# A hybrid decoder layer: projections that hand TensorE over at every second group of three matmuls

## The chip, the core and the metric

One core of a Trainium2 chip runs the whole layer as one program. The metric is the device time of one execution in microseconds (us), the median of several runs. The engines are named as the profile names them: PE is TensorE (PEld its weight loads), DVE VectorE, ACT ScalarE, POOL GpSimd, SP SyncE, whose queue issues most of the DMAs.

## What is computed

The input x is 512 tokens of 2048 numbers, all in float32. With the modulation left out, the layer is:

```
h = rmsnorm(x) * (1 + sc_m) + sh_m
proj = h @ w_in                      # 2048 x 8208
o_hg  = hgrn2_group(proj[:, :4096])  # 8 heads: q, f, i, g of 128 columns each
o_gdn = gdn_group(proj[:, 4096:])    # 8 heads: q, k, v, g of 128 columns each
y = concat(o_hg, o_gdn) @ w_out
x = x + gt_m * rmsnorm(y)
...                                  # then the MLP with w_ff1 and w_ff2
```

Each HGRN2 head is a gated linear recurrence over the tokens. Each Gated DeltaNet head needs a triangular solve for every chunk and then a recurrence from chunk to chunk:

```
v_new = u_c - w_c @ S
o = qd_c @ S + qk_c @ v_new
S = S * tail + kt_c^T @ v_new
```

## The kernel before, in words

Large products run as three matmuls for each pair of 128x128 weights and 128x512 activations: every float32 operand is split into a high part H and a low part L, and `mm3` issues H·H, H·L and L·H into one PSUM bank. A group of three matmuls below is one call of `mm3`. The weights come by DMA into `raw` tiles of 128x1024; ACT makes the high part (`wh`, L197) and DVE the low part (`wl`, L199), each split feeding eight groups.

The stage that the change touches is called the mixing here. It lasts from about 285 to 1095 us of the profiled execution. Its parts on TensorE are:

- Projections. For heads 2 to 7 there are eight columns per head, 48 in all, and `project` (L933) runs 16 groups for each into a bank `pj` (three banks). Then `out_mm` groups of the output projection follow (banks `pout`).
- The recurrences, in three threads, each a Python generator that yields the time that its next step should wait. `solve_thread` runs the triangular solve of one DeltaNet head: the matmuls `pk`, `pkk` and `pb`, and then 15 steps of substitution that are DVE work alone (L1032 and L1034, tiles `utmp` and `uc`). `gdn_thread` runs the rest of that head: `pqk`, two levels (`py`, `pz`), then four chunks with the matmuls `p1` (from the state S), `p2`, `p4` and `po`, and at the end four transposes `pog`. `hg_thread` runs an HGRN2 head: `pd`, seven levels `pa`, then chunks `hp` and `hpo`, and the transposes `poh`. The trace leaves numbers out, so `p1`, `p2` and `p4` are all `p` there and are told apart by what they read (S, R or U, vn).

Between two matmuls of one thread lies work on DVE, ACT and POOL. For one `p1` it is the update of S on DVE (L1146).

What sets the order: PE and SP are in program order (`manual_schedule`), and `run` writes that program. It keeps a clock of its own. It takes the first thread whose next step is due by that clock, and if none is due it takes one step of the filling work, `fill`, that is the projections and then the output projection. A step of a projection ends where the generator `project` yields, so a recurrence that falls due during a step waits until its end. DVE, ACT and POOL are ordered by the framework's scheduler, which follows the program, so their order moves with it.

At the end of the mixing `fill_thread` starts the output projection. Its last two pairs of heads need the transposes of DeltaNet head 7 (`pog7`, then L957 into `xo`, and the split of it into `oH` on ACT, L1418, and `oL` on DVE, L1419) and of HGRN2 head 7 (`poh7`, likewise).

Of the kernel before, what the change touches and what calls it, by code (L numbers as in the profile page):

```python
# [235 lines left out]
def hybrid_layer_kernel(  # L236
# [228 lines left out]
    def mm3(ps, aH, aL, bH, bL, start, stop):  # L465
        mm(ps, aH, bH, start, False)
        mm(ps, aH, bL, False, False)
        mm(ps, aL, bH, False, stop)
# [436 lines left out]
    def pj(name):  # L905
        return bank("pj", name)
# [26 lines left out]
    def project(col, out):  # L933
        ps = pj(f"pj{col}")
        for hf in range(2):
            wH, wL = ws.get(("in1", col, hf))
            for kk in range(8):
                kt = hf * 8 + kk
                mm3(ps, wH[:, kk, :], wL[:, kk, :], hH[:, kt, :], hL[:, kt, :], kt == 0, kt == KT - 1)
                yield 0  # L940
        out.append(ps)

    def finish_head(name, slot, osb, sso, nw, gate, rq=None):
# [415 lines left out]
    def fill_thread():  # L1359
# [29 lines left out]
        for h in range(2, NH):  # L1389
            todo = [(("grec", h - 2), gpre, C_GK, None), (("grec", h - 2), gpre, C_GQ, None),  # L1390
                    (("v", h - 1), gpre, C_GV, ("gpre", h)),
                    (("hrec", h - 1), hpre, C_HF, None), (("hrec", h - 1), hpre, C_HQ, None),
                    (("hv", h - 1), hpre, C_HI, ("hpre", h)),
                    (("gfin", h - 1), gpre, C_GG, ("gate_g", h)), (("hfin", h - 1), hpre, C_HG, ("gate_h", h))]
            for need, f, cc, tok in todo:
                yield from flush(PJ - 1)
                out = []
                yield from project(cc + h * P, out)
                pending.append((need, f, cc, h, out.pop(), tok, True))
# [404 lines left out]
```

## Time and profile before

| | |
|---|---|
| median of 3 runs | 2586.42 us (2584.91 to 2587.82) |
| the profiled execution's own time | 2583.66 us |
| its span in the profile | 2581.9 us |
| PE busy | 2469.1 us, 96% of the span, 12627 instructions |
| DVE busy | 1875.9 us, 73% |
| ACT, POOL busy | 1118.1 us (43%), 1032.4 us (40%) |
| DMA | 350.64 MB, 136 GB/s on the mean |

To read it: the page gives busy time per engine over the whole span, but the stages differ. In the MLP, from about 1262 to 2470 us, PE has no idle time at all; in the start and the mixing it has. So a share over the span says little about the mixing, and the rows further down are of that stretch. A matmul of 128x512 shows some 390 ns, but matmuls are pipelined and follow each other about every 227 ns. The idle time in brackets in a row of the timeline is the time in which the engine did nothing before that instruction, and behind the arrow stands what ended the wait.

### The profile page before, as it was taken

Reading aid. Unit: us, or ns where it says so; the run is one execution under the profiler, and the core shown is the slowest. Engines: PE = TensorE matmul, PEld = TensorE weight load, DVE = VectorE, ACT = ScalarE, POOL = GpSimd, SP = SyncE. Lnnn points to the kernel's source line nnn. Section 1 sums busy time; section 2 is a strip of 40 time slices with the busy share of each in tenths; the row PEclk is TensorE's granted clock in tenths of the full one; section 3 lists DMA queues with packets and bytes.
Section 4 is the critical chain, followed back from the end, with each engine's and each line's share of the span. In section 5 each row is a group of like instructions: output and inputs, shape, how many; then the busy total and the mean of one; then the engine's idle time right before and its main releaser. Section 6 shows DMA issues by size and latency. Waiting matters only on the chain.

```text
span 2581.9 us, 34110 instructions
## 1 busy us (share of the span) xinstructions
PE 2469.1 (96%) x12627; PEld 2007.2 (78%) x12627; DVE 1875.9 (73%) x2709; ACT 1118.1 (43%) x1765; POOL 1032.4 (40%) x646
## 2 busy tenths in 40 slices
PE   5889999998999899999999999999999999999998
PEld 3667777777777778788788888888888888888876
DVE  7997877768586765634668776777768777677787
ACT  5553544544444452423444444444434434443333
POOL 5561344445444440000244535445354444533333
PEclk9999999999999999999999999999999999999999
DMA  8762434444545432344423332433424333232334
GB/s 320 255 203 74 128 119 147 139 148 138 160 142 164 139 115 82 130 140 155 154 98 133 104 135 95 146 123 106 142 95 139 110 127 135 94 114 82 122 116 161
DMA packets 127300, 350.64 MB, mean 136 GB/s; under 512 B 14247, under 2 KB 18713, under 8 KB 125981
## 3 DMA queue, kind: packets, MB, share of 16 engines
q1 hardware_dynamic: 126938, 348.41, 40.0%
q8 instruction: 99, 1.62, 0.3%
q14 instruction: 67, 0.55, 0.1%
q10 hardware_dynamic: 196, 0.06, 0.0%
HBM read 340.01 MB, written 8.40 MB: 135 GB/s over the span
## 4 chain that ended last, share of the span: by engine, by line
PE 67%; DVE 6%; POOL 1%; ACT 1%; issue 1%; DMA 1%; DVEq 0%; ACTq 0%; POOLq 0%
PE pf L331 27%; PE pg L331 22%; PE pj L331 9%; PE pout L331 7%; DVE wl L199 1%; DVE uc L1034 1%; PE pa L331 1%; DVE utmp L1032 1%; POOL y L1728 0%; POOL aacc L451 0%; PE p L331 0%; DVE x2r L1746 0%; DMA ada<-in_w_ada_dram 0%; DVE zkT L493 0%; PE pz L331 0%
## 5 line engine op out<-in xcount | busy, mean ns | idle before, releaser
L199 DVE TENSOR_TENSOR wl<-raw,wh 128x1024 fp32r<-128x1024 f32 x506 | 720.1, 1424 | 427.8 <-ACT wh L197 422.6
L197 ACT CAST wh<-raw 128x1024 fp32r<-128x1024 f32 x512 | 538.0, 1052 | 943.4 <-PE pf L331 285.9
L165 POOL TENSOR_TENSOR raw<-raw,raw 128x1024 f32<-128x1024 f32 x150 | 438.9, 2941 | 392.7 <-DMA raw<-in_w_ff_dram 181.6
L331 PE MATMUL pf<-h2L,wh 128*128 128x512 f32 x1024 | 399.9, 391 | 0.0
L331 PE MATMUL pf<-h2H,wh 128*128 128x512 f32 x1024 | 399.7, 390 | 0.0
L331 PE MATMUL pf<-h2H,wl 128*128 128x512 f32 x1024 | 399.6, 390 | 0.0
L451 POOL TENSOR_TENSOR aacc<-ada,aacc 128x512 f32<-128x512 f32 x180 | 268.9, 1494 | 253.5 <-ACT ada L449 242.2
L331 PE MATMUL pg<-wl,cH 128*128 128x512 f32 x840 | 327.6, 390 | 1.1 <-DVE wl L199 1.1
L331 PE MATMUL pg<-wh,cL 128*128 128x512 f32 x840 | 327.3, 390 | 0.0
L331 PE MATMUL pg<-wh,cH 128*128 128x512 f32 x840 | 327.3, 390 | 0.0
L331 PE MATMUL pj<-hH,wh 128*128 128x512 f32 x768 | 325.2, 423 | 0.0
L331 PE MATMUL pj<-hH,wl 128*128 128x512 f32 x768 | 305.0, 397 | 4.4 <-DVE wl L199 4.4
L331 PE MATMUL pj<-hL,wh 128*128 128x512 f32 x768 | 304.0, 396 | 0.0
L331 PEld LDWEIGHTS pf<-h2H,wh 128*128 128x128 f32 x1024 | 192.7, 188 | 39.7
L331 PEld LDWEIGHTS pf<-h2L,wh 128*128 128x128 f32 x1024 | 192.7, 188 | 39.6
L331 PEld LDWEIGHTS pf<-h2H,wl 128*128 128x128 f32 x1024 | 192.7, 188 | 39.6
L451 POOL TENSOR_TENSOR gacc<-ada,gacc 128x512 f32<-128x512 f32 x64 | 108.4, 1694 | 278.9 <-ACT ada L449 278.9
L1627 DVE TENSOR_TENSOR y<-pg,y 128x512 f32<-128x512 f32 x344 | 219.0, 682 | 0.0
L331 PEld LDWEIGHTS pg<-wl,cH 128*128 128x128 f32 x840 | 157.8, 188 | 35.0 <-DVE wl L199 2.3
L331 PEld LDWEIGHTS pg<-wh,cH 128*128 128x128 f32 x840 | 157.8, 188 | 32.7
L331 PEld LDWEIGHTS pg<-wh,cL 128*128 128x128 f32 x840 | 157.8, 188 | 32.5
L331 PEld LDWEIGHTS pj<-hH,wl 128*128 128x128 f32 x768 | 146.4, 191 | 39.2 <-DVE wl L199 6.5
(434 smaller groups left out, 3770.3 us busy)
## 6 DMA issues: line engine op xcount, KB each, us to landing
raw<-in_w_ff_dram SPq DMA_DIRECT2D x256, 512.0 KB, 4.0
raw<-in_w_in_dram SPq DMA_DIRECT2D x128, 512.0 KB, 3.4
ada<-in_w_ada_dram SPq DMA_DIRECT2D x256, 256.0 KB, 3.4
adas<-in_w_ada_dram SPq DMA_DIRECT2D x128, 256.0 KB, 4.4
raw<-in_w_out_dram SPq DMA_DIRECT2D x40, 512.0 KB, 3.5
xo<-in_x_dram SPq DMA_DIRECT2D x8, 512.0 KB, 9.4
xr<-in_x_dram SPq DMA_DIRECT2D x8, 512.0 KB, 6.8
x2d<-z SPq DMA_DIRECT2D x4, 1024.0 KB, 5.7
```

The lines of the kernel that those rows point to most:

```text
L165: self.nc.gpsimd.tensor_tensor(out=out, in0=ra, in1=rb, op=op)
L197: self.cast = self.nc.scalar.copy(out=h, in_=raw).ins
L199: eng.tensor_tensor(out=lo, in0=raw, in1=h.bitcast(F32), op=ALU.subtract)
L331: nc.tensor.matmul(ps, lhsT=lhsT, rhs=rhs, start=start, stop=stop)
L451: nc.gpsimd.tensor_tensor(out=acc, in0=a, in1=acc, op=ALU.add)
L1032: nc.vector.tensor_tensor(out=tmp[:, :, :n], in0=xj, in1=uc[:, :, j : j + 1].broadcast_to([P, NCH, n]), op=ALU.mult)
L1034: nc.vector.tensor_tensor(out=uc[:, :, j + 1 :], in0=uc[:, :, j + 1 :], in1=tmp[:, :, :n], op=ALU.subtract)
L1627: nc.vector.tensor_tensor(out=dst, in0=ps, in1=dst, op=ALU.add)
```

## The change

`project` yields after every second group in place of every one, so `run` looks for a recurrence that is due half as often:

```
--- before.py
+++ after.py
@@ -937,7 +937,8 @@
             for kk in range(8):
                 kt = hf * 8 + kk
                 mm3(ps, wH[:, kk, :], wL[:, kk, :], hH[:, kt, :], hL[:, kt, :], kt == 0, kt == KT - 1)
-                yield 0
+                if kk % 2:
+                    yield 0
         out.append(ps)
```

The matmuls are the same, 10187 rows on PE in both programs, and so is their order outside the mixing. Inside it the recurrences' steps stand at other places between the projections. The runs of projection matmuls between recurrence steps go from 225 to 197 in number; the shortest has six matmuls where it had three.

The first place is the wait for the solve of a DeltaNet head, on PE, head 6. The solve's last matmul `pb6` comes earlier; shown is the piece from `pqk6` to the first level `py6_4` (`pj768` is a projection, `Ud6` what the solve yields). The dots stand for more rows of the same projection, 6 before and 9 after. Before:

```order
L331 MATMUL pqk6_8407<-qT6_8151,kT6_7964 128x128 x4
L331 MATMUL pj768_8384<-hH_95,wh104_8333 128x512
L331 MATMUL pj768_8384<-hL_96,wh104_8333 128x512
L331 MATMUL pj768_8384<-hH_95,wl104_8334 128x512
...
L331 MATMUL py6_4_8424<-Ud6_8403,Ap6_8105 64x64 x8
```

After:

```order
L331 MATMUL pqk6_8428<-qT6_8097,kT6_7940 128x128 x4
L331 MATMUL pj768_8378<-hH_95,wh105_8381 128x512
L331 MATMUL pj768_8378<-hL_96,wh105_8381 128x512
L331 MATMUL pj768_8378<-hH_95,wl105_8382 128x512
...
L331 MATMUL py6_4_8466<-Ud6_8424,Ap6_8129 64x64 x8
```

Nine projection matmuls stood between the two and twelve do now; from `pb6` to `py6_4` it is 69 and 84.

The second place is on DVE, head 0, at the update of the state that the third chunk's `p1` reads (`S0_1`; `wl36` is a weight split, `E1`, `gsc1`, `QP1` and `KS1` are work of head 1's solve and levels). Before:

```order
L987 TENSOR_TENSOR E1_2905<-E1_2905,gcum_111 128x512
L1188 COPY_PREDICATED hd1_2936<-lmask1_88,pa1_1_3022 128x256
L1198 TENSOR_TENSOR QP1_2788<-QP1_2788,tot1_0_2974 128x128x2
L1200 TENSOR_TENSOR KS1_2782<-KS1_2782,tot1_0_2974 128x128x2
L199 TENSOR_TENSOR wl36_3039<-raw36_2856,wh36_3038 128x1024
L1146 SCALAR_TENSOR_TENSOR S0_1_3062<-S0_0_2950,tl_114,p4_0_1_3060 128x128
```

After:

```order
L1201 TENSOR_TENSOR KS1_2782<-KS1_2782,tot1_0_2977 128x128x2
L985 TENSOR_TENSOR gsc1_3002<-gsc1_3002 128x4
L1204 TENSOR_TENSOR tot1_2_3119<-tot1_1_3058 128x64
L986 SCALAR_TENSOR_TENSOR gsc1_3002<-gsc1_3002,eg_112 128x4
L988 TENSOR_TENSOR E1_2911<-E1_2911,gcum_111 128x512
L1147 SCALAR_TENSOR_TENSOR S0_1_3093<-S0_0_2959,tl_114,p4_0_1_3091 128x128
```

The weight split has left the place just ahead of the update; the last one now stands 12 rows ahead.

The third place is the end of the mixing on PE, at the transposes of DeltaNet head 7 (`pout0_0` is the output projection; `wh134` are the weights of the pair that contains head 7, `wh132` those of an earlier pair). Before:

```order
L342 MATMUL pog7_10161<-ident_69,at7_9486 128x128 x4
L331 MATMUL hp4_7_1_10167<-hvk7_10087,hk7_10115 128x128
L331 MATMUL hpo7_1_10171<-hvk7_10087,hat7_9725 128x128
L331 MATMUL hpo7_1_10171<-hS7_0_10143,QP7_9571 128x128
L331 MATMUL pout0_0_9976<-wh132_10129,oH_185 128x512
```

After:

```order
L342 MATMUL pog7_10235<-ident_69,at7_9507 128x128 x4
L331 MATMUL hpo7_3_10241<-hvk7_10102,hat7_9720 128x128
L331 MATMUL hpo7_3_10241<-hS7_2_10222,QP7_9553 128x128
L331 MATMUL pout0_0_9934<-wh134_10204,oH_185 128x512
L331 MATMUL pout0_0_9934<-wl134_10205,oH_185 128x512
```

The transposes have moved down to just ahead of the matmuls that need their result: three matmuls on head 6 come first, and the fourth reads head 7.

## Rows read from the trace of the kernel before

**Rows 1.** Windows by stage: stretch, its length, busy time by engine, PE clock, DMA.

```profile
285.00:1095.00 810.00, 769.54 (x4879) 616.18 (x4877) 577.95 (x1120) 373.25 (x770) 332.17 (x261) 0.99 0.42 136
1262.00:2470.00 1208.00, 1208.00 (x5333) 1001.02 (x5332) 881.77 (x935) 507.16 (x578) 535.22 (x212) 1.00 0.34 117
```

**Rows 2.** Waits of PE, 285 to 1095 us: total us, times, longest.

```profile
PE p L331 <- DVE S L1146: 8.5, 5, 2.6
...
PE pa L331 <- DVE KS L1200: 2.0, 2, 1.3
```

**Rows 3.** Chain that ended last, 960 to 980 us: start, us, what.

```profile
964.92 9.55 PE pj L331 x42
```

**Rows 4.** Timeline of PE: the waits of py for the solve.

```profile
358.54 0.68 PE L331 MATMUL py<-Ud,Ap 64*64 64x64 f32 x16 [2.98 <-DVE xo L957]
...
630.53 0.68 PE L331 MATMUL py<-Ud,Ap 64*64 64x64 f32 x16 [2.20 <-DVE Ud L1050]
...
754.02 0.68 PE L331 MATMUL py<-Ud,Ap 64*64 64x64 f32 x16 [1.54 <-DVE Ud L1050]
...
877.63 0.68 PE L331 MATMUL py<-Ud,Ap 64*64 64x64 f32 x16 [3.79 <-DVE Ud L1050]
```

**Rows 5.** Timeline of PE: the longest waits of p1, and of pog and poh.

```profile
322.59 0.79 PE L331 MATMUL p<-S,kT 128*128 128x128 f32 x2 [2.12 <-DVE S L1146]
...
410.97 0.49 PE L331 MATMUL p<-S,kT 128*128 128x128 f32 x2 [1.84 <-DVE S L1146]
...
496.28 0.49 PE L331 MATMUL p<-S,kT 128*128 128x128 f32 x2 [2.56 <-DVE S L1146]
...
613.08 0.66 PE L342 MATMUL pog<-ident,at 128*128 128x128 f32 x2 [3.38 <-DVE at L952]
...
855.18 0.90 PE L342 MATMUL poh<-ident,hat 128*128 128x128 f32 x3 [2.87 <-DVE hat L952]
```

**Rows 6.** Windows after waits, columns as in rows 1.

```profile
322.61:326.02 3.41, 3.41 (x22) 2.78 (x23) 3.31 (x8) 0.40 (x2) 0.80 (x1) 0.50 0.70 253
...
878.98:882.39 3.41, 3.41 (x9) 2.64 (x9) 3.38 (x7) 0.00 (x0) 1.39 (x1) 0.50 0.61 187
630.53:633.94 3.41, 3.41 (x28) 2.87 (x29) 3.41 (x5) 0.00 (x0) 2.33 (x2) 1.00 0.48 135
```

**Rows 7.** Timeline of PE: a recurrence step between projections, and two steps side by side.

```profile
1040.41 0.39 PE L331 MATMUL p<-S,kT 128*128 128x128 f32 x2
1040.73 0.69 PE L331 MATMUL pa<-QP,KS 128*64 128x64 f32 x16
...
1043.55 0.38 PE L331 MATMUL p<-R,U 128*128 128x128 f32 x2
1043.69 0.48 PE L331 MATMUL pj<-hH,wh 128*128 128x512 f32 x1
1044.01 0.40 PE L331 MATMUL pj<-hL,wh 128*128 128x512 f32 x1
```

**Rows 8.** Timeline of DVE ahead of the update that ends at 322.5 us.

```profile
319.99 2.30 DVE L199 TENSOR_TENSOR wl<-raw,wh 128x1024 fp32r<-128x1024 f32 x1
322.21 0.33 DVE L1146 SCALAR_TENSOR_TENSOR S<-S,tl,p 128x128 f32<-128x128 f32 x1
```

**Rows 9.** Timeline of DVE in the substitution of head 6.

```profile
872.94 2.42 DVE L1034 TENSOR_TENSOR uc<-uc,utmp 128x12 f32<-128x12 f32 x1
875.40 0.17 DVE L1032 TENSOR_TENSOR utmp<-X,uc 128x8 f32<-128x8 f32 x1
```

**Rows 10.** Timeline of PE, ACT and DVE from the transposes of HGRN2 head 7.

```profile
1086.68 0.60 PE L342 MATMUL poh<-ident,hat 128*128 128x128 f32 x4
...
1088.11 0.62 ACT L1418 CAST oH<-xo 128x512 fp32r<-128x512 f32 x1
...
1088.01 1.23 DVE L199 TENSOR_TENSOR wl<-raw,wh 128x1024 fp32r<-128x1024 f32 x1
1089.15 0.68 DVE L1419 TENSOR_TENSOR oL<-xo,oH 128x512 fp32r<-128x512 f32 x1
```

## The prediction

> **What bounds the kernel now.** I read the windows by stage first. In the MLP PE is busy for the whole of its 1208 us, so nothing can be won or lost there; in the mixing it is busy for 769.5 of 810 us [rows 1]. So PE bounds this stage too, but 40.5 us of it are idle. The planner always has projections to put in, so these idle times are no lack of work: PE stands at a recurrence's matmul whose input isn't ready and can't go past it. Next I read the list of PE's waits in that stretch: nearly all name DVE, and the largest sums belong to the p that reads the state, 8.5 us in five waits [rows 2], and to py, four waits of 2.98, 2.20, 1.54 and 3.79 us, 10.5 together [rows 4]. Then come one pog with 3.38 and one poh with 2.87 [rows 5]. DVE itself is busy for 578 of the 810 us [rows 1], so it isn't the bound on the mean; it is late at some places.
>
> A wait has a second price. After seven of the waits the granted clock is 0.50, the lower of the two levels, 1.2 GHz, for 3.41 us, and after the 2.20 us before the py at 630.53 it stays at 1.00 [rows 6] (the first and the last of the seven, and the one without). All seven follow or end a wait of PE of 1.84 us or more. With PE busy at half pace 3.41 us lose 1.7 us of work, so seven cost 12 us beside the 40.
>
> What counts is the **cover**: the projections between two steps of a thread. One matmul is worth 9.55/42 = 0.227 us [rows 3], three are 0.68, six 1.36.
>
> **The change part by part.** Nothing is added or removed on any engine: PE, the DMAs, the weight splits and the DVE work keep their number; only their order in the mixing moves. The SP queue's order moves with it (weights, conditioning weights, the decay rows of the next head), at no cost in my sum: no wait of PE on a DMA stands among the waits of this stretch that I read, and the weights are requested ahead of their use; if that cover went, each late weight would stop PE as the splits do now, for up to 1.8 us.
>
> 1. *Fewer switches: 0.* The runs of projections go from 225 to 197. After a recurrence step the first projection takes 0.32 us to the next start instead of 0.227, 0.09 more; 28 times that would be 2.5. But two recurrences side by side pay it among themselves: the p ahead of a pa takes 0.32 us, ahead of a projection 0.14 [rows 7]. Steps of two threads that stand side by side go from 50 to 74 in PE's order, and 24 times 0.09 gives 2.2 back. I take 0, bounds -2.5 and +2.2.
>
> 2. *Waits of py for the solve: -8.5.* The substitution is a chain on DVE, and the planner spreads four waits over it, each of which now ends at a coarser step. So the cover from pb to py grows: head 1 from 63 matmuls to 72, head 4 from 69 to 90, heads 5 and 6 from 69 to 84. By 0.227 this is 2.05, 4.78 and twice 3.41 us against the waits of 2.98, 2.20, 1.54 and 3.79 [rows 4]: 2.05 + 2.20 + 1.54 + 3.41 = 9.2 go. Head 3 falls from 78 to 72, 1.36 us; it waits for nothing today, and I charge half, 0.7. Bounds: -10.5, all of it, and +1.4, no relief and all of head 3.
>
> 3. *Waits of p1 for the state: -2.7.* Here the cover hardly changes, six matmuls in most places before and after; what changes is what stands in front on DVE. At 322.59 a weight split of 2.30 us ended just ahead of the update [rows 8]; now the split is 12 rows away, which is worth the whole wait of 2.12 [rows 5]. At 410.97 it was 4 rows away and is 13; I take half of 1.84, 0.9. At 496.28 the split still stands just ahead: the 2.56 stay. The other two waits, together 8.5 - 6.5 = 2.0, lose about 1.0, since one gets three matmuls more of cover and the other loses its split. Against this, heads 3, 5, 6 and 7 have six matmuls ahead of their third chunk where they had nine, without a wait now: four times 0.68, half of it, +1.4. Bounds -8.5 and +2.7.
>
> 4. *Ends of the heads: -3.4.* Between the last chunk of DeltaNet head 3 and pog there are 54 matmuls instead of 42, 2.7 of its 3.38 us; for HGRN2 head 5 it is 48 for 45, 0.7 of 2.87 [rows 5]. Bounds -6.2 and 0.
>
> 5. *Low clock: -5.1.* By terms 2 to 4 five of the seven waits ahead of a low clock shrink below 1.84: those at 322.59, 358.54, 410.97, 613.08 and 877.63. I count three times 1.7, since a wait of two microseconds sometimes leaves the clock alone [rows 6]. Bounds -8.5 and 0.
>
> 6. *New waits: +6.7.* Steps of two threads that fall due together put their DVE work one behind the other, and the trace of before doesn't show those places. The nearest rows are the waits inside recurrences, 8.5 for p and 2.0 for pa [rows 2]; grown as the side-by-side steps do, by 24/50, they add 5.0, and one more low clock 1.7. Bounds: 0, and 24 new waits of the mean 8.5/5 = 1.7, which is 41.
>
> 7. *End of the mixing: +1.4.* The recurrences end later against the projections, so the transposes of DeltaNet head 7 now stand just ahead of their users. From the start of such a transpose the ACT half is there after 1088.73 - 1086.68 = 2.05 us and the DVE half, behind a split of 1.23, after 3.15 [rows 10]; 3.35 with a copy that now stands between. PE covers the rest of the transposes, two small steps and three matmuls, 1.5 us, then two more matmuls before the one that reads the DVE half, 0.45. It lacks 1.4. The later poh7 has 18 matmuls of cover instead of 30, still 4.1 us, and I charge nothing. Bounds 0 and 3.35.
>
> The sum: 0 - 8.5 - 2.7 - 3.4 - 5.1 + 6.7 + 1.4 = -11.6. The profiled execution took 2583.66 us, so it would take 2572.1; it lies 2.76 below the median of the runs, and against that median the forecast is **2574.8**.
>
> **The rivals.**
>
> *The waits only move.* DVE's queue is redrawn over the whole stage, and 40 us of waits in other places may again be 40. For it: nothing takes work off DVE, and most waits are coincidences on its queue. Against it: the py waits come from a chain whose cover grows in four heads by 2 to 5 us. Terms 2 to 6 would sum to 0 and term 7 stay: 2587.8.
>
> *DVE stretches with the cover.* One update of the substitution took 2.42 us where its neighbour took 0.17 [rows 9], and a split 2.30 beside 1.23 for one of the same shape [rows 8, 10]. If in the 3.41 us of new cover two more updates are stretched by 2.25, the chain grows as fast as its cover: term 2 is 0, two of the three low clocks stay, and the sum is -2.7 - 3.4 - 1.7 + 6.7 + 1.4 = +0.3, 2586.7. Against it: the chain has as many other DVE rows and weight splits between its steps as before (118 rows and 16 of them splits for head 6, before and now). The Trainium skill (SBUF — State Buffer, section Who interferes with whom) has a rule that makes this: a VectorE instruction with two SBUF inputs and a GpSimd instruction that reads SBUF exclude each other, and the later one waits in full. The stretched rows agree with it; by that rule cover on PE doesn't shorten the chain, and the time would be this rival's.
>
> *Slower: the side-by-side steps meet short covers.* The place is the p1 with six matmuls ahead, 1.36 us. Where an HGRN2 step now goes just ahead of a p4, its DVE work stands ahead of the state's update. Without term 6 the sum is -18.3, and a new wait costs 1.7: from 11 of the 24 new pairs on the gain is gone, from 14 on the kernel is slower by over 5.2. With 16 it would be +8.9, or 2595.3. For it: three of the p1 waits arose in just this way, behind another thread's work. Against it: the wait of a thread's next step grows by half a step on the mean, too, and many of the pairs meet steps with long cover.
>
> **How the numbers follow.** A measurement of this kernel tells about 0.2%, 5.2 us, from no change. The forecast gets 0.64; I count 0.03 of it within 0.2%, with few waits relieved. Waits that only move get 0.15, the stretched chain 0.09, the slower case 0.12. So faster 0.61, same 0.03 + 0.15 + 0.09 = 0.27, slower 0.12. The range: with five low clocks less, no new wait and no stop at the end it would be -8.5 - 2.7 - 3.4 - 8.5 = -23.1, or 2563.3, and I start at 2563. Upwards it takes in the two cases of no change and ends at 2589; the slower case lies outside.
>
> **What would show it.** The four py rows shrink to two short ones (term 2), or show the same idle time behind stretched utmp and uc rows. The p at heads 0 and 1 have no wait ahead of the third chunk, that at head 2 keeps its own (3). The pog of head 3 waits under 1 us (4). Windows at 0.50 in the mixing are three or four (5). New rows in the list of waits, or longer ones for pa and hpo, are term 6. At pog7 PE waits for oL for over 1 us (7). The prediction is wrong if idle time in the mixing stays at 40 us, or if the low clock comes as often after shorter waits.

## The result, and the profile after

The changed kernel took **2601.65 us** (median of 4 runs, 2601.01 to 2602.25), the kernel before, run beside it, 2587.12 us (2584.91 to 2588.05). The ratio is 1.0059, with a 95% interval of 1.0047 to 1.0072: 14.5 us slower, where the forecast was 2574.8 and faster. The profiled execution took 2601.93 us, its span is 2600.2 us.

Windows by stage of the changed kernel; they answer to [rows 1], with the same columns. The mixing now runs to 1113 instead of 1095 us:

```profile
285.00:1113.00 828.00, 775.65 (x4880) 622.46 (x4879) 578.36 (x1120) 370.98 (x770) 338.05 (x261) 0.97 0.41 133
1280.00:2488.00 1208.00, 1207.95 (x5332) 1000.33 (x5331) 888.85 (x934) 506.93 (x577) 533.04 (x212) 1.00 0.34 117
```

The MLP is as it was. In the mixing PE is idle for 828.00 - 775.65 = 52.4 us, where it was 40.5, and its mean clock there fell from 0.99 to 0.97. The whole loss lies in this stage.

Waits of PE in the mixing after the change, total us, times, longest; they answer to [rows 2]:

```profile
PE pj L331 <- DVE wl L199: 14.1, 7, 4.7
PE hp L331 <- DVE hS L1231: 6.6, 2, 3.4
PE hpo L331 <- DVE hat L1241: 5.8, 5, 1.7
PE p L331 <- DVE R L1132: 5.0, 3, 2.6
PE pa L331 <- DVE hd L1178: 4.8, 1, 4.8
PE py L331 <- DVE xo L958: 3.5, 2, 2.7
PE pa L331 <- DVE KS L1201: 3.4, 1, 3.4
...
PE p L331 <- DVE S L1147: 1.3, 1, 1.3
PE pgw L331 <- DVE hgate L506: 1.1, 1, 1.1
...
PE pog L342 <- DVE at L953: 0.7, 1, 0.7
```

(Lines from 941 on have moved down by one.) The waits that the prediction wanted to remove are mostly gone: the p that reads S has 1.3 us left of 8.5 [rows 2], pog 0.7 of 3.38 and poh none of 2.87 [rows 5]. Other rows have taken their place, above all the projection's own weight split (wl) and HGRN2's chunk steps (hp, hpo).

Two of py's waits are left. Timeline of PE, to be read beside [rows 4]:

```profile
363.11 0.39 PE L331 MATMUL py<-Ud,Ap 64*64 64x64 f32 x6 [2.72 <-DVE xo L958]
...
455.76 0.45 PE L331 MATMUL py<-Ud,Ap 64*64 64x64 f32 x8 [0.77 <-DVE xo L958]
```

One of the new waits, and DVE's queue ahead of it (timelines of PE and of DVE in the changed kernel; the columns are start, us, engine, line, operation):

```profile
852.60 0.80 PE L331 MATMUL hp<-hvk,hk 128*128 128x128 f32 x2 [3.39 <-DVE hS L1231]
```

```profile
843.64 1.26 DVE L949 TENSOR_TENSOR rsg<-sso,rqs 128x4 f32<-128x4 f32 x1
844.94 0.16 DVE L950 TENSOR_TENSOR rsg<-rsg,rqs 128x4 f32<-128x4 f32 x1
845.14 1.15 DVE L426 TENSOR_SCALAR rsg<-rsg 128x4 f32<-128x4 f32 x1
847.42 0.16 DVE L952 TENSOR_TENSOR rsg<-rsg,rqs 128x4 f32<-128x4 f32 x1 [1.14 <-POOL rsg L427]
847.62 0.69 DVE L953 TENSOR_TENSOR at<-at,rsg 128x512 f32<-128x512 f32 x1
848.23 0.68 DVE L979 TENSOR_TENSOR kt<-pk,ekt 128x512 f32<-128x512 f32 x1
...
850.11 0.17 DVE L983 TENSOR_TENSOR gsc<-gsc,beta 128x4 f32<-128x4 f32 x1 [1.12 <-POOL gsc L427]
...
850.79 1.55 DVE L988 TENSOR_TENSOR E<-E,gcum 128x512 f32<-128x512 f32 x1
852.27 0.28 DVE L1231 COPY hS<-hp 128x128 f32<-128x128 f32 x1
```

DVE works its rows off in order. The copy of HGRN2's first chunk (hS, 0.28 us) stands behind the end of DeltaNet head 5 (rsg, at) and the start of the solve of head 6 (kt, gsc, E), 8.6 us from 843.64 to 852.27, in which the queue stands still twice for over 1.1 us until POOL has a root ready. A head later the same pattern comes again: PE waits 3.24 us at 976.38.

The clock after such waits, columns as in [rows 6], four of the nine stretches at 0.50 in the mixing:

```profile
364.26:367.67 3.41, 3.36 (x19) 2.69 (x19) 1.31 (x5) 2.09 (x5) 1.32 (x2) 0.50 0.12 44
541.75:548.57 6.82, 6.27 (x28) 4.97 (x29) 1.58 (x5) 0.08 (x1) 0.00 (x0) 0.50 0.43 154
852.37:855.78 3.41, 3.18 (x15) 3.18 (x16) 1.24 (x4) 3.40 (x8) 0.00 (x0) 0.50 0.00 0
975.25:982.07 6.82, 5.69 (x20) 5.03 (x21) 4.65 (x8) 3.44 (x7) 2.00 (x2) 0.50 0.00 1
```

Before there were seven stretches of 3.41 us; after there are five of 3.41 and four of 6.82, 44.4 us in all. PE was busy for 38.4 us of these, and loses half of that, 19.2 us, where it lost 11.7 before. So in the profile: idle time +11.9, clock +7.5, PE's own work 1 us less. Together that is the 18.3 us by which the two spans differ (the two profiled executions stand a little further apart than the medians).

By place, most of it comes early. From the first projection to `pqk` of DeltaNet head 5 (749.3 us before, 765.0 after) the idle time grew from 27.8 to 36.2 us and the loss to the clock from 8.4 to 13.1; from there on they grew from 12.8 to 16.2 and from 3.4 to 6.1. So two thirds of the loss lie ahead of the chunk steps of heads 5 and 6 that the rows above show. The longest waits in the early part are these (timeline of PE):

```profile
542.30 0.48 PE L331 MATMUL pa<-QP,KS 128*64 128x64 f32 x4 [4.76 <-DVE hd L1178]
...
643.20 0.79 PE L331 MATMUL pj<-hH,wl 128*128 128x512 f32 x1 [4.71 <-DVE wl L199]
...
741.16 0.80 PE L331 MATMUL pj<-hH,wl 128*128 128x512 f32 x1 [3.65 <-DVE wl L199]
```

Ahead of the first two DVE's queue again has the end of a DeltaNet head (rsg, its root from POOL, at), from 535.47 and from 635.58 us on.

### The profile page after: what moved, and what is told of

Its sections match the earlier page's. It is cut to its first block, busy times and chain, and to the rows that moved or that the text cites. A ratio compares the mean times of both kernels' runs of the same rounds, so it can differ in the third digit from the quotient of the medians.

```text
span 2600.2 us, 34104 instructions
## 1 busy us (share of the span) xinstructions
PE 2476.9 (95%) x12627; PEld 2013.3 (77%) x12627; DVE 1882.3 (72%) x2709; ACT 1116.4 (43%) x1765; POOL 1036.3 (40%) x646
## 4 chain that ended last, share of the span: by engine, by line
PE 78%; DVE 15%; POOL 3%; issue 2%; ACT 2%; DMA 1%; SPq 0%; DVEq 0%; ACTq 0%; POOLq 0%
PE pf L331 27%; PE pg L331 22%; PE pj L331 13%; PE pout L331 7%; DVE wl L199 3%; DVE asum L440 2%; PE pph L331 1%; PE pa L331 1%; PE accg L331 1%; DVE utmp L1033 1%; DVE uc L1035 1%; PE ppg L331 1%; POOL aacc L451 1%; DVE zqT L493 1%; PE pz L331 1%
## 5 line engine op out<-in xcount | busy, mean ns | idle before, releaser
L451 POOL TENSOR_TENSOR aacc<-ada,aacc 128x512 f32<-128x512 f32 x180 | 274.3, 1524 | 262.3 <-ACT ada L449 254.8
L331 PE MATMUL pj<-hH,wl 128*128 128x512 f32 x768 | 306.9, 400 | 14.1 <-DVE wl L199 14.1
```

The costliest lines, as they stand in the source:

```text
L331: nc.tensor.matmul(ps, lhsT=lhsT, rhs=rhs, start=start, stop=stop)
L451: nc.gpsimd.tensor_tensor(out=acc, in0=a, in1=acc, op=ALU.add)
```

## The experiments

Two columns of this table are summed up from the traces, from the first projection of the mixing to the last matmul of the output projection: PE's idle time, and half of the time for which it was busy at 0.50. What is left of the stretch, PE's work at full pace, is 884 to 894 us in all twenty rows, 890.6 in the kernel before: these two columns are most of the difference between the kernels. The ratio is against the kernel before, run on the same chip beside it.

| run | median us | ratio, 95% interval | PE idle, us | lost to the clock, us |
|---|---|---|---|---|
| before | 2587.12 | | 40.3 | 11.7 |
| after | 2601.65 | 1.0059 (1.0047 to 1.0072) | 52.2 | 19.2 |
| e1 other phase | 2607.55 | 1.0091 (1.0076 to 1.0106) | 56.5 | 17.8 |
| e2 every 4th | 2578.43 | 0.9975 (0.9965 to 0.9984) | 38.2 | 9.7 |
| e3 coarse, apart | 2599.57 | 1.0055 (1.0038 to 1.0072) | 49.0 | 19.8 |
| e4 fine, apart | 2610.51 | 1.0099 (1.0084 to 1.0114) | 62.7 | 13.7 |
| e5 hS first | 2604.53 | 1.0071 (1.0054 to 1.0088) | 57.4 | 14.7 |
| e6 wl first | 2611.08 | 1.0097 (1.0082 to 1.0113) | 60.0 | 19.5 |
| e7 fine, 1.53 | 2589.60 | 1.0012 (1.0002 to 1.0022) | 45.5 | 9.4 |
| e8 fine, 1.61 | 2593.74 | 1.0029 (1.0017 to 1.0040) | 50.6 | 13.0 |
| e9 chunks held | 2605.26 | 1.0071 (1.0054 to 1.0088) | 52.5 | 20.9 |
| e10 before, late | 2594.20 | 1.0031 (1.0019 to 1.0043) | 46.5 | 17.6 |
| e11 coarse, 1.40 | 2589.78 | 1.0016 (1.0006 to 1.0025) | 46.4 | 10.0 |
| e12 after, no additions | 2544.49 | 0.9839 (0.9825 to 0.9854) | 14.8 | 0 |
| e13 before, no additions | 2528.93 | 0.9780 (0.9766 to 0.9795) | 0.9 | 0 |
| e14 every 4th, no additions | 2539.33 | 0.9823 (0.9808 to 0.9838) | 10.2 | 3.3 |
| e15 before, additions on DVE | 2555.20 | 0.9885 (0.9870 to 0.9900) | 21.1 | 4.4 |
| e16 every 8th | 2646.66 | 1.0238 (1.0221 to 1.0255) | 66.4 | 53.7 |
| e17 after, additions on DVE | 2562.71 | 0.9910 (0.9894 to 0.9927) | 24.3 | 6.4 |
| e18 as e15, longer solve waits | 2556.24 | 0.9887 (0.9871 to 0.9903) | 21.2 | 5.8 |

### Side by side, or a new draw: e1 to e4

My first theory was the prediction's term 6 in a stronger form: steps that fall due at one hand-over meet on DVE, and 26 more such pairs cost 15 us (82 steps before and 108 after follow a step of another thread directly; the prediction counts side-by-side steps more narrowly, 50 and 74). The edits of e1 and e2, shown against the changed kernel:

```diff
-                if kk % 2:
+                if kk % 2 == 0:        (e1)
+                if kk % 4 == 3:        (e2)
```

> The projection hands over after groups 0, 2, 4 and 6 of each eight instead of 1, 3, 5 and 7: the same grain as the changed kernel, the other phase. In PE's order 108 steps of the recurrences still follow a step of another thread directly, as in the changed kernel (82 in the kernel before). Theory 'side by side' (steps of two threads that fall due at one hand-over queue up on DVE, 26 more such pairs cost the 15 us, 0.6 each): 2601, within 4. Theory 'redraw' (the coarse grain costs nothing of itself, the changed kernel's order is an unlucky one): anywhere from 2575 to 2600, centred on 2587.

> The projection hands over after every 4th group of three matmuls. 139 steps follow a step of another thread directly. Side by side: 31 pairs more than in the changed kernel at 0.6 us each, so 2620, at least 2608. Redraw: centred on 2587 again, 2575 to 2600.

```diff
-            if t is not None:
+            ready = fill is not None and (fill[1] is None or fill[1] in tokens)
+            if t is not None and not (turn and ready and slack == SLACK):
+                was = clock[0]
                 v = next(t[0], "end")
+                turn = clock[0] > was
...
```

(e3 on the changed kernel, e4 on the kernel before.)

> The changed kernel, and after a step of a recurrence the planner puts in a piece of projection (two groups) before the next step, when there is one to put in. 43 steps still follow a step of another thread directly, most of them at the end where no projection is left; the grain stays at two groups. Side by side: the loss goes and some of the waits that the kernel before has too, so 2587 less 39 pairs at up to 0.6 us, 2564 to 2585. Redraw: centred on 2587, 2575 to 2600. A third theory, 'late steps' (a coarse grain makes each thread's own steps late, which no order of two threads mends): 2600 or more, since the steps come later still.

> The kernel before, with the same rule: after a step of a recurrence a piece of projection (here one group) comes before the next step. 31 steps still follow a step of another thread directly, instead of 82. Side by side: 51 pairs fewer at up to 0.6 us, 2557 to 2580. Redraw: centred on 2587, 2575 to 2600. Late steps: 2587 to 2592.

The theory fell. The grain with the most pairs (e2, 139) is the fastest of the six orders so far, and the two with the fewest (43 and 31) are slower than the kernel before. The other phase of the same grain costs 6 us more than the change. The theory of late steps came near in e3 (2599.6 for 2600 or more) and failed in e4 (2610.5 for 2587 to 2592). So neither the number of pairs nor the size of the piece orders the times, and e1 and e4 even lie outside what I had given to a plain new draw: the kernel before is better than most of its neighbours.

### One row in front: e5 and e6

Here PE's order stays row for row. The edits aim at DVE's order; some rows of ACT move with it.

```diff
+                with tc.high_priority():
-                if ch == 0:
+                    if ch == 0:                                        (e5: hS, L1231 and L1233)
...
+        with self.first():                                             (e6: wl, L199, in the mixing)
-        eng.tensor_tensor(out=lo, in0=raw, in1=h.bitcast(F32), op=ALU.subtract)
+            eng.tensor_tensor(out=lo, in0=raw, in1=h.bitcast(F32), op=ALU.subtract)
```

> The changed kernel with the update of the HGRN2 state (hS, L1231) ranked ahead of other ready work when DVE's order is made. PE's order stays as it is, row for row; on DVE 14 rows move, among them hS of heads 5 and 6, which now stands ahead of five rows of the next DeltaNet head's solve. Theory 'one row in front' (each new wait of the changed kernel is made by what happens to stand just ahead on DVE's in-order queue): the waits of hp for hS, 3.39 and 3.24 us, go, and with them the low clock after them, 3.41 and 6.82 us at 0.50, which costs half: 6.6 + 5.1 = 11.7 less, 2590, within 4. Rival 'cover' (the DVE work between two steps is too much for the projections ahead of the step, in whatever order it stands): the wait turns up at the next rows, the copies of hat or the solve's products, and the time stays at 2601, within 3.

> The changed kernel with the low parts of the weight splits (wl, L199) ranked ahead of other ready work on DVE in the mixing; PE's order stays, on DVE 95 rows move. One row in front: the 14.1 us of pj waiting for wl go, with the low clock after the ones of 4.71, 3.65 and 2.26 us (6.82, 6.82 and 3.41 us, half of it 8.5); against it, each split put ahead of a recurrence's row can delay that by up to 2.3 us, which I take at half the gain: 2590, 2579 to 2601. Cover: 2601, within 5, with the waits at the recurrences' steps instead of at pj.

e5 missed its target: what moved was the update of the third chunk, while the waits are for the copy of the first chunk, which stayed where it was (hp waits 6.7 us for hS, 6.6 without the edit). It says nothing about that row; the time stayed where it was, within the intervals of the two ratios. e6 hit its target and was slower by 9 us than the changed kernel: of the 14.1 us for wl 9.0 stayed, in three waits instead of seven, and p waits 8.8 us for R. Two long waits that the changed kernel doesn't have came besides, 4.8 us of pb for rsh and 4.4 of pa for sc1f. What the splits gained in front was lost again in the recurrences.

### The grain of before at other waits: e7 and e8

```diff
-SLACK = 1.57
+SLACK = 1.53        (e7; 1.61 in e8)
```

> The kernel before at its own grain, one group, with the factor on the recurrences' waits (SLACK) at 1.53 instead of 1.57. 84 steps follow a step of another thread directly (82 before). Theory 'redraw' (any new order of PE draws the waits anew; the order of the kernel before is a good draw): 2590 to 2610. Theory 'grain' (the number of groups to a piece makes the difference): 2586, within 4, since the grain is that of the kernel before.

> The kernel before at its own grain with the factor at 1.61. 81 steps follow a step of another thread directly. Redraw: 2590 to 2610, and not the same as with 1.53. Grain: 2586, within 4.

Between the two theories: 3 and 7 us slower than the runs of the kernel before beside them. The fine grain stays within 8 us of its best over this range, the grain of two groups lay at 2600 to 2608 in three orders. That was a hint that the coarse grain had something of its own against it, and no proof, since e4 has the fine grain and took 2610. I looked for what it could be.

### Where the two threads stand to each other: e9 to e11

Each step of a thread comes late by half a piece on the mean, by half of three more matmuls, 0.34 us, when the piece grows from three to six. Between pqk and pog DeltaNet has 21 waits of the planner, HGRN2 from pd to hpk 9. In head 5 the stretch from pqk to pog grew from 81.6 us (749.3 to 830.9) to 92.2 us (765.0 to 857.2), the one from pd to hpk from 42.1 to 44.6. So DeltaNet fell back against HGRN2: the first chunk step of HGRN2 came 11 us after DeltaNet's last in heads 5 and 6, and now comes 5.0 us after it, into the burst of DVE rows shown above. In heads 4 and 7 it comes 0.1 and 3.2 us after, and waits 1.3 us and not at all.

```diff
-        yield 1.5
+        yield 1.5 + 4.0 * (h in (5, 6))                            (e9, changed kernel, behind hk, L1219)
...
-        yield 2.0
+        yield 2.0 + 4.0 * (h in (5, 6))                            (e10, kernel before, L1118)
         tokens.add(("levels", h))
```

> The changed kernel with one wait longer: in HGRN2 heads 5 and 6 the chunk steps start 6.3 us later (4.0 times the factor 1.57). In PE's order the projections between DeltaNet's last chunk (po3) and the first HGRN2 chunk (hp4) grow from 4.1 to 9.5 us in these two heads, which is what the kernel before has there. Theory 'offset' (the coarser piece lengthens DeltaNet's chain of a head from 81.6 to 92.2 us and HGRN2's hardly, so that the end of a DeltaNet head, a burst of work on DVE, falls onto HGRN2's chunk steps, in every head again): the waits of hp and hpo in heads 5 and 6, 6.3 and 4.0 us, and half of the low clock behind them, 3.41 and 6.82 us, go: 15.4 less, 2586, within 5. Rival 'burst' (DVE is behind for longer than 6 us there, the chunk steps meet the solve's rows instead): 2598 to 2605.

> The kernel before with one wait longer: in DeltaNet heads 5 and 6 the chunk loop starts 6.3 us later. The projections between po3 and the first HGRN2 chunk shrink from 9.5 to 3.4 us, near the 4.1 us of the changed kernel; the grain stays at one group. Offset: hp and hpo wait 4 to 6 us in each of the two heads, and low clock follows: 10 + 5 more, 2597 to 2602. Rival 'grain' (the waits come from the coarse piece, not from where the two threads stand): 2587, within 4.

> The changed kernel with the factor on the recurrences' waits at 1.40 instead of 1.57, which takes back on the mean what the coarser piece adds to each wait. The projections between po3 and the first HGRN2 chunk are 6.8, 8.2 and 4.1 us in heads 4, 5 and 6 (0, 4.1 and 4.1 in the changed kernel; 12.9, 9.5 and 9.5 before). Offset: head 5 comes clear, head 6 keeps its waits, 8 less: 2594, within 6. Grain: 2601, within 4. Redraw: anything from 2578 to 2610.

e10 confirms that an offset of some 4 us makes these waits. With the first chunk 4.0 us behind po3, hp waits for hS twice, in the order of the kernel before, for 7.8 us, where the changed kernel has 6.6 (waits of PE in e10):

```profile
PE p L331 <- DVE S L1146: 9.1, 4, 2.6
PE hp L331 <- DVE hS L1230: 7.8, 2, 3.9
```

The time rises by 8.3 us against the runs beside it, somewhat less than I expected; these 7.8 us are the largest new group of waits. Up to the chunk loop of head 5 e10 has the order of the kernel before on every engine, row for row. Yet its profiled execution is 3.9 us behind at `pqk` of head 5, 1.1 idle and 2.9 by the clock, with two waits that the other execution lacks (timeline of PE in e10):

```profile
333.96 0.49 PE L331 MATMUL p<-S,kT 128*128 128x128 f32 x2 [2.59 <-DVE S L1146]
...
437.19 0.42 PE L331 MATMUL pa<-QP,KS 128*64 128x64 f32 x7 [3.16 <-DVE uc L1034]
```

So one wait of 2 or 3 us in one trace is not yet a property of an order. From `pqk` of head 5 on e10 has 5.0 us more idle time and 2.9 more lost to the clock.

An offset of 4 to 6 us is enough for such waits, but not needed. Of the fine-grained orders, e4 has 15 us between the two threads in heads 4 to 6 and waits 7.3, 6.7 and 4.6 us at the chunk steps there, and e8 has 17.6 us in head 4 and waits 7.9.

e9 shows that the offset is not all of the loss: it took 2605.3, as its rival 'burst' said, and not 2586. With the chunks held back, 11.8 us behind `po3`, the waits of hp and hpo in heads 5 and 6 fell from 10.3 to 4.4 us, and the time did not fall. The projections wait longer for the weight splits instead (waits of PE in e9; 14.1 and 6.6 us in the changed kernel):

```profile
PE pj L331 <- DVE wl L199: 18.3, 9, 4.7
...
PE hp L331 <- DVE hS L1231: 3.8, 2, 2.5
```

In e11, where the shorter waits give back on the mean what the coarse piece adds, the coarse grain comes to 2589.8, 4 us above the runs of the kernel before beside it. Its head 5 stands at 13.3 us and doesn't wait at the chunk steps, its head 6 at 6.0 and waits 3.4 us there, as expected. But this factor moves every step of the mixing, so the 12 us that it gains on the changed kernel aren't the offset's alone.

### What makes DVE late: e12 to e14

These three leave the 180 additions of the mixing out (`left_out` is set there alone). e12 is the changed kernel without them, e13 the kernel before, e14 the hand-over at every 4th group.

```diff
-        if not first:
+        if not first and not left_out:
             nc.gpsimd.tensor_tensor(out=acc, in0=a, in1=acc, op=ALU.add)
```

> The changed kernel without the 180 additions on POOL that sum up the conditioning weights during the mixing (274 us of POOL's time; the output then lacks these sums, so this is no version of the kernel). PE's and DVE's orders stay as they are, row for row. Theory 'stretched rows' (what makes DVE late is that its rows stand still beside POOL: rsg took 1.26 us where a row of its shape takes 0.16, and wl 2.30 where it takes 1.22): half of the 52 us of idle PE in the mixing goes, and half of the 22 us lost by low clock: 26 + 11 less, 2565, 2555 to 2580. Rival 'the queue alone' (the order of the rows and the two round trips to POOL for the roots make it late, POOL's additions don't): 2596 to 2603.

> The kernel before without the 180 additions on POOL in the mixing (its output lacks those sums, as in the run of the changed kernel without them, which took 2544.5). Theory 'stretch alone' (the two orders of PE differ only in which rows of DVE happen to meet POOL's additions): 2544, within 4, and no difference between the two grains is left. Theory 'order' (the coarse order is worse by itself): 2530, the 15 us stay. Theory 'prediction' (the relieved waits of py, p1 and pog would have paid, had nothing been stretched): 2549 to 2560, slower than the changed kernel without the additions.

> The kernel that hands over after every 4th group, without the 180 additions on POOL in the mixing (its output lacks those sums). Stretch alone: 2543, within 4: with the additions it was 23 us faster than the changed kernel, and that difference goes too. Order: 2521, the 23 us stay. A theory 'coarser is better' would keep a part of them.

This is the pair that settled most. Windows of the mixing without the additions, in the changed kernel (e12) and in the kernel before (e13), columns as in [rows 1]:

```profile
285.00:1056.00 771.00, 756.04 (x4886) 610.49 (x4885) 478.22 (x1122) 374.09 (x771) 62.87 (x81) 1.00 0.42 143
```

```profile
285.00:1042.00 757.00, 755.90 (x4904) 610.55 (x4899) 483.04 (x1124) 376.68 (x773) 65.95 (x82) 1.00 0.43 146
```

PE's order is that of the kernel with the additions, row for row, and DVE's too but for four rows in e13. 57.2 us went from the changed kernel (2601.65 to 2544.49) and 57.2 from the kernel before (2586.13 beside it to 2528.93); for e12 I had expected 37, at most 47. The clock stays at 1.00. And the difference between the two orders is still there: 15.6 us. PE's waits in the mixing, e12 first, then e13:

```profile
PE hpo L331 <- DVE hat L1243: 6.8, 5, 2.2
PE p L331 <- DVE R L1134: 2.3, 2, 1.9
PE pj L331 <- DVE wl L199: 1.4, 1, 1.4
PE pgw L331 <- DVE hgate L508: 1.1, 1, 1.1
PE hp L331 <- DVE hS L1233: 1.0, 2, 0.5
```

```profile
PE pout L331 <- ACT oH L1422: 0.3, 1, 0.3
PE pog L342 <- DVE at L954: 0.2, 1, 0.2
...
PE p L331 <- DVE S L1148: 0.2, 1, 0.2
```

That is the reading I had missed. In the order of the kernel before *every* step is covered: when POOL's additions don't stretch DVE's rows, PE waits for 1.1 us in 757 (757.00 - 755.90). The 40 us of waits that the prediction set out to shorten were not too little cover but stretched rows. The changed order has waits of its own, 15.0 us, and over half of them (6.8 + 1.0) stand at HGRN2's chunk steps, where DeltaNet has slid onto them: with the additions gone its head 5 still takes 86.7 us from pqk to pog, against 78.7 in e13, and the first chunk stands 5.0 us behind po3, against 11.3. The two differences of some 15 us, with the additions and without, are alike in size but not in make: without them 4.6 us of it stand ahead of `pqk` of head 5 and 9.2 behind, and none is the clock's. That the changed order is worse in both cases is shown, that it is so by the same waits is not.

The stretch itself, groups of DVE rows in the mixing, mean ns behind the busy time; the changed kernel, then e12:

```profile
L1201 DVE TENSOR_TENSOR KS<-KS,tot 128x256 f32<-128x256 f32 x38 | 28.9, 761 | 0.0
...
L1189 DVE COPY_PREDICATED hd<-lmask,pa 128x256 f32<-128x256 int16 x40 | 17.9, 447 | 21.0 <-PE pa L331 20.8
```

```profile
L1191 DVE COPY_PREDICATED hd<-lmask,pa 128x256 f32<-128x256 int16 x42 | 18.7, 446 | 29.3 <-PE pa L331 29.1
L1203 DVE TENSOR_TENSOR KS<-KS,tot 128x256 f32<-128x256 f32 x42 | 18.7, 446 | 0.0
```

KS, which reads two tiles in SBUF, falls from 761 to 446 ns without POOL's additions; hd, whose data come from PSUM, stays at 447 and 446. With fewer rows to do POOL might also answer DVE sooner, and that could have been the gain; but in the mixing DVE stands idle for POOL for 32.5 us in 29 waits before and for 30.9 in 30 without the additions, while DVE's busy time falls from 577.95 us [rows 1] to 483.04. The Trainium skill (SBUF — State Buffer, section Who interferes with whom) has this rule: a VectorE instruction with two SBUF inputs contends with a GpSimd instruction that reads SBUF, one with at most one SBUF input does not, outside its two-port modes. The trace agrees.

e14 shows that every 4th group isn't a better order: it gained only 39.1 us by the removal, and without the additions it is 10 us behind the kernel before. Its 0.25% hung on which rows met the additions. What the additions cost an order is thus not a constant either, though it was the same for before and after.

### A cheaper place for the additions, and the coarsest grain: e15 to e18

```diff
-            ada_pool(tiles.pop((seg, cb, r)), 512, r, 1, acc, r == 0, ws.cast)
+            with tc.issue_after(ws.cast):
+                ada_vector(tiles.pop((seg, cb, r)), 512, r, 1, acc, r == 0)      (e15; with the change e17)
```

> The kernel before with the additions of the conditioning weights in the mixing on DVE (one multiply-add each, about 0.75 us by the rows of that shape that nothing stretched), instead of a scaling on ACT and an addition on POOL. DVE gets 180 x 0.75 = 135 us of work more in the mixing and loses the stretch, about 60 us by the run without the additions. PE's order stays. Stretch: POOL's additions cost some 42 to 57 us, rows of 0.75 us in the queue cost less; 2570, within 12. Rival 'load' (what counts is how much DVE has to do in all): 2600 or more.

> The changed kernel with the additions of the conditioning weights on DVE, as in the run of the kernel before that took 2555.2. Theory 'order' (the coarse order carries its 15 us of waits with it, whatever stretches DVE's rows): 2570, within 5. Theory 'cover' (in that run py waits 12.3 us for the solve in four places, which the coarse order covers by 2 to 5 us more each): 2546 to 2553. Theory 'stretch alone': 2555, within 4.

One fused row on DVE in place of a scaling on ACT and an addition on POOL. The group of these rows in e15 and the two longest groups of waits of PE there:

```profile
L440 DVE SCALAR_TENSOR_TENSOR aacc<-ada,c,aacc 128x512 f32<-128x512 f32 x180 | 137.5, 764 | 46.4 <-DMA ada<-in_w_ada_dram 45.6
```

```profile
PE py L331 <- DVE Ud L1050: 12.3, 4, 4.7
PE p L331 <- DVE S L1146: 3.6, 4, 1.1
```

DVE has 137.5 us more to do, and PE waits half as long as in the kernel before: how much DVE has to do was not the point, the stretch was. (e15 also takes the scalings off ACT; what part of the gain that is no run separates.) At **2555.2 us**, 1.15% less than the kernel before, this is the fastest version of this study beside those that leave the sums out. The change on top of it (e17) costs 7.5 us: py's 12.3 us do go, as the prediction says they should, but 6.2 us for hat, 4.4 for hd and 3.5 for R come in their place. That lies outside all three ranges, halfway between "stretch alone" (2555) and "order" (2570).

```diff
             if j % 4 == 3:
-                yield 2.0
-        yield 2.0
+                yield 2.4
+        yield 2.4
```

> The kernel before with the additions on DVE, and each of the planner's waits over the substitution (L1037, L1038) at 2.4 instead of 2.0: five waits, 3.1 us more cover from pb to py, with the grain left at one group. The four waits of py, 4.67, 2.28, 0.80 and 4.55 us, fall to about 1.6, 0, 0 and 1.5: 9 less, and the low clock behind the two long ones, 5.1 lost in all, goes: 2555 - 9 - 5 = 2541. Against it, DeltaNet's head ends 2 to 3 us nearer to HGRN2's chunk steps (8 instead of 10 us of projections between): theory 'offset' gives back 4 to 8 there, 2545 to 2549. Theory 'redraw' (the waits come up elsewhere): 2555 to 2565.

The cover for py alone, at the grain of before, on top of e15: 2556.2, no gain. Waits of PE in e18:

```profile
PE py L331 <- DVE Ud L1050: 5.8, 2, 4.1
PE p L331 <- DVE S L1146: 5.3, 4, 2.6
PE p L331 <- DVE S L1144: 4.0, 2, 2.5
```

There are four such waits of the planner and not five, and the cover grew by 1.4 to 2.7 us instead of 3.1. py's waits fall from 12.3 to 5.8, and S takes most of the difference, from 3.6 to 9.3 us. The time is within the range of "redraw", at its lower end.

```diff
-                if kk % 2:
+                if kk == 7:        (e16, against the changed kernel)
```

> The projection hands over once per eight groups, that is between the halves of a projection. 168 steps follow a step of another thread directly, the projections come in 108 runs (234 before). Redraw: 2575 to 2610. A theory 'coarser is better beyond two groups' (every 4th took 2578): 2575 or less. A theory 'late steps' (each step comes up to 5.4 us late, and the ends of the heads hold the projections up): 2610 or more.

At 2646.7 late steps win. In the trace the stage is 62.5 us longer than before: 26.1 are idle time, 42.0 the clock, and PE's own work is 5.5 less. So the clock costs more than the waits here. That eight groups are too coarse is shown; a rule for sizes in between is not.

## Why the prediction was wrong

**Fewer switches (0, bounds -2.5 and +2.2).** PE's own work fell by 1 us in the profile of after (890.8 to 889.7), within the bounds; without the additions it rose by 1.7 (886.1 to 887.8).

**py (-8.5).** 10.5 us fell to 2.72 + 0.77 = 3.5: -7.0. Heads 4, 5 and 6 went as worked out. In head 1, where I had 2.05 us of relief from nine matmuls, 2.72 of 2.98 stayed, now behind the end of the head before it.

**p1 for S (-2.7).** 8.5 fell to 1.3: -7.2. But R, which the same chunk loop needs next, waits 5.0 us where it had no row before, so the chunk loop as a whole gave 2.2 (these 5.0 are counted below, with the new waits).

**pog and poh (-3.4).** 3.38 + 2.87 fell to 0.7: -5.6.

**End of the mixing (+1.4).** oL lacks 0.5 us, not 1.4; oH and aacc lack 0.6 each, of which 0.7 in all was there before, and pgw waits 1.1 us for hgate: +2.1.

**Low clock (-5.1).** The sign was wrong: +7.5. Four of the five waits I named did shrink below 1.84; others came, nine waits of 2.26 to 4.76 us now have such a stretch behind or around their end, and at four of them it is 6.82 us long, a length that the mixing of the kernel before doesn't have.

**New waits (+6.7, of which 5.0 idle).** This is the step that failed. All of the idle time outside the places above was 40.5 - 10.5 - 8.5 - 3.38 - 2.87 - 0.7 = 14.5 us and became 52.4 - 3.5 - 1.3 - 0.7 - 2.8 = 44.1: +29.6. I had scaled the waits that I saw (8.5 and 2.0) by the number of side-by-side steps, and e2 to e4 show that this number carries nothing. In its place the runs show waits at steps that had little or none: wl 14.1 us where it had 4.4, HGRN2's chunk steps in heads 5 and 6 10.3 where they had none, R 5.0, hd 4.8. For the chunk steps I could have seen it coming by following both threads through a head. 21 late steps against 9 move DeltaNet's end by some 4 us or more against HGRN2's chunks, which stood 11 us clear of it; the burst of DVE rows at a head's end is 8 us long. For the waits at wl, R, hd and KS, which make up most of the new waits ahead of head 5, the rows show at two places that the end of a DeltaNet head stands ahead of them too, and no experiment tests it. The bound of 41 for this term did hold what came, the value taken was at the wrong end of it.

Behind that stands a second error, of reading. I took the waits of the kernel before for places where cover was short. Cover was hardly short anywhere: without the additions no wait behind the kernel before's order is longer than 0.3 us in the mixing (e13). The second rival, stretched rows, had the right mechanism for the waits: nearly all of the 40 us of the kernel before, and the low clock behind them, hang on POOL's additions (e13). But I let it act only on the solve, priced at 12 us, and gave it 9 in 100. The rival that ended slower had the right sign, and with work of another thread ahead on DVE the right kind of wait. But it put it at p1, whose waits for S fell, and priced it by the number of pairs; its 2595.3 was short by 6 us.

Not settled: of the 15 us of waits that the changed order has without the additions 7.8 stand at chunk steps, and that an offset like its own makes such waits is shown (e10); the others, at R, at the split and at the end, are seen but were not tested one by one. With the additions the larger part of the loss lies ahead of head 5, and no experiment takes its waits apart. That e9 did not pay is explained by where its waits went, not by an experiment of its own.

## What to carry to other kernels

Before a new order is priced by the waits that it removes, ask what made these waits: leave the suspected stretcher out of the old order once, and if the waits vanish, the old order had cover enough. A retiming then has little cover to win, and what it changes is above all which rows get stretched. When each step of several threads is delayed by the same small amount, add it up along each thread: the thread with more steps slides against the others, and a collision at one place can come back in later rounds, as here in heads 5 and 6. An accumulation on GpSimd beside a busy VectorE can cost more than doing it on VectorE: here 180 additions, with their scalings, moved to the busier engine gave 31 us.

## What was not expected of the hardware

The additions are 274 us of work on an engine off the critical path, and taking them out of the mixing gave 57 us. The stretch reaches rows of almost no work: rsg with 128x4 elements took 1.26 us (two SBUF inputs) and 1.15 us (TENSOR_SCALAR, one input) in the rows above. The one-input row is stretched as well, so hd's case isn't that of every row with one input; in which mode it ran no row shows. The same two in e12 (timeline of DVE):

```profile
796.01 0.15 DVE L951 TENSOR_TENSOR rsg<-sso,rqs 128x4 f32<-128x4 f32 x1
...
796.40 0.17 DVE L426 TENSOR_SCALAR rsg<-rsg 128x4 f32<-128x4 f32 x1
```

On the clock: waits in e12 of 1.91, 2.16 and 2.16 us were followed by no stretch at 0.50 at all, while all nine waits of 2.26 us and more in the changed kernel came with 3.41 or 6.82 us of it, and in the kernel before one of 1.84 did [rows 5, 6]: a wait of two microseconds is no sure price for the clock, which the prediction allowed for by charging three low clocks for five waits. Nor does the length of the wait decide: in e14 waits of 1.47 and 1.33 us were followed by 3.41 us at 0.50, in e11 one of 3.54 us by none.
